# A gated delta rule in a hybrid decoder block: the block inverses leave through ScalarE's queue, the first chunk's apart and first

## The chip, the cores and the metric

One core of a Trainium2 chip runs one program. The metric is the device time of one execution in microseconds (us), median of several runs, lower is better. The core's engines are TensorE (PE), VectorE (DVE), ScalarE (ACT), GpSimd (POOL) and SyncE (SP); SyncE computes nothing and issues transfers. Each engine works through its own queue in order.

## What is computed

One decoder block in float32 for 1024 tokens of 1024 features. The normed input goes through one projection; one group of heads does sparse attention, the other the gated delta rule; both results go through an output projection, a second norm, a gated feed-forward layer and a last norm. The change touches the delta rule. The reference, cut to that part (chunks of 64 tokens there):

```python
a = jnp.where(strict, jnp.einsum('nbhcd,nbhed->nbhce', kb, k) * decay, 0.0)
tmat = lax.linalg.triangular_solve(a + eye, eye, left_side=True, lower=True, unit_diagonal=True)
u = tmat @ (v * beta[..., None])
w = tmat @ (kb * jnp.exp(gc)[..., None])
def step(S, xs):
    q_i, k_i, u_i, w_i, gc_i, qk_i = xs
    v_new = u_i - w_i @ S
    o = (q_i * jnp.exp(gc_i)[..., None]) @ S + qk_i @ v_new
    S = S * jnp.exp(g_last) + jnp.einsum('bhck,bhcv->bhkv', k_i * jnp.exp(g_last - gc_i)[..., None], v_new)
    return S, o
```

The triangular inverse `tmat` of each chunk must be there before the chunk's first step; the state `S` makes the steps a chain over the chunks.

## The kernel before

The kernel works with 8 chunks of 128 tokens and 4 heads, so 32 triangular matrices of 128 x 128. They are inverted in two stages. First the 32 x 32 blocks on their diagonals, 4 in each of 32 matrices, are inverted all at once: each of the 128 partitions holds one block. Then each chunk's blocks are joined to a 128 x 128 inverse by TensorE.

The order in the source is this. `gdn_proj` projects and convolves q, k and v feature block by feature block and writes them to `gD` in DRAM. `gram(c)` makes a chunk's triangular matrices and writes them to `gaD`, and the masked products of q and k to `gqD`. Then comes the inversion of the diagonal blocks: `bd` is read back from `gaD` through `diag_view`, which puts one block on each partition; 31 rounds of two VectorE operations (L574, L576) build the inverse in `xi`; `xi` is written to `uD` (L577); VectorE copies it transposed into a second tile under the tag "bd" (L579); that goes to `tD` (L580). Each row of 32 numbers is one run of 128 bytes in DRAM, so each of the two writes has 4096 runs. `uD` and `tD` were filled with zeros before (L398), 4 writes each, so that the parts off the diagonal read as zero. All these transfers are issued by SyncE.

The scan has two classes. `Inv.load(c)` reads a chunk's `u0` and `t0` (L636, L637) and then three pieces of `gaD` (L640, L643); `i1` to `i4` join the blocks, and `i1` (helper line L617) needs `t0`. `Scan.s0(c)` reads q, k (L503) and v (L686), transposes v and k with 8 matmuls (L625) and scales them with 8 ScalarE copies (L691, L697). `s1` to `s4` are the chunk's step, `rest` its output. `ORDER` interleaves the stages of chunk c with the inverse of chunk c + 1, and `seq` chains their matmuls in that order on TensorE. For chunk 0 the source has the load, `i1` to `i4`, and after them `s0`.

What runs beside it: projections for the attention heads (`proj_tok`), written after the scan in the source, fill TensorE while the inversion runs. A projection takes 8 token blocks of 24 matmuls; each block ends in one of 2 PSUM banks "mm", ScalarE evicts it (L812 for keys, L827 for queries) into one of 2 tiles "kst", GpSimd rotates it (L317 to L322), SyncE writes it out (L814 to `kD`, L829 to `qD`). New weights come through `wprep` (L203 read, L205 ScalarE copy, L208 GpSimd remainder).

The order on each engine is not the source's: the framework builds the queues ahead of the run by playing the program through with estimated times, taking what is ready and, of several, what stands first in the source. A wait at the head of a queue holds everything behind it. Tiles of a pool take addresses that earlier pools gave back; a tile waits for the tiles that lay there. Before, `xi`, `bd` and `tmp` lie in the pool `pg` on the left side, whose place the scan's pool `ph` takes when `pg` closes.

Of the kernel before, what the change touches and what calls it, by code (L numbers as in the profile page):

```python
# [79 lines left out]
def hybrid_block(ctx, tc, xT, xN, pos, cst_d, vec_d, w_tok, w_gdn, cw1, cw2, cpos, w_out, w_gu, w_dn, out):  # L80
# [7 lines left out]
    def mk(pool, shape, tag, dtype=F32, bufs=1):  # L88
        return pool.tile(list(shape), dtype, name=nm(tag), tag=tag, bufs=bufs)

    def pool(name, side=None, space=None):
        st = ExitStack()
        kw = {} if space is None else {"space": space}
        p_ = st.enter_context(tc.tile_pool(name=name, bufs=1, side=side, reuse_waits="tile", **kw))
        return p_, st
# [4 lines left out]
    def bc(ap, shape):  # L100
        return ap.to_broadcast(list(shape))
# [31 lines left out]
    def dram(shape, tag):  # L133
        return mk(dr, shape, tag)
# [2 lines left out]
    gD = dram([12, P, T], "gD")  # L137
    zD = dram([NT, P, 512], "zD")
    gaD = dram([NT * 4, HS], "gaD")
    uD = dram([NT * 4, HS], "uD")  # L140
    tD = dram([NT * 4, HS], "tD")
    gqD = dram([NT, P, 4, P], "gqD")
    mgD = dram([P, 2, 4, T], "mgD")
    kD = dram([NT, P, 256], "kD")
# [6 lines left out]
    def chunk_view(d, c):  # L151
        return d[c * 4:(c + 1) * 4, 0:P * P].rearrange("h (s t) -> s h t", t=P)

    def diag_view(d):
        return bass.AP(tensor=d.tensor, offset=d.offset, ap=[[HS // 4, P], [P, 32], [1, 32]])


    pc = ctx.enter_context(tc.tile_pool(name="pc", bufs=1))
# [233 lines left out]
    zz = mk(p1, [P, 1032], "zz")  # L392
    G.memset(zz, 0.0)
    for d in (uD, tD):
        zv = d.rearrange("(p a) (b f) -> p (a b) f", a=1, b=4)
        zv = bass.AP(tensor=d.tensor, offset=d.offset, ap=[[4 * 1032, P], [1032, 4], [1, 1032]])
        for b in range(4):
            dma(zv[:, b, :], zz)  # L398
    p1_x.close()
    psa_x.close()  # L400

# [160 lines left out]
    V.scalar_tensor_tensor(out=fv, in0=ssk, scalar=0.5, in1=rk, op0=ALU.mult, op1=ALU.mult)  # L562


    bd = mk(pg, [P, 32, 32], "bd")
    dma(bd, diag_view(gaD))
    xi = mk(pg, [P, 32, 32], "xi")
    G.memset(xi, 0.0)
    G.memset(xi.rearrange("p a b -> p (a b)")[:, 0:1024:33], 1.0)
    for r in range(31):  # L570
        n = 31 - r
        tmp = mk(pg, [P, 256], "tmp", F32, 2)
        tv = tmp[:, 0:(r + 1) * n].rearrange("p (a b) -> p a b", b=n)
        V.tensor_tensor(out=tv, in0=bc(xi[:, 0:r + 1, r:r + 1], [P, r + 1, n]),  # L574
                        in1=bc(bd[:, r:r + 1, r + 1:32], [P, r + 1, n]), op=ALU.mult)
        V.tensor_tensor(out=xi[:, 0:r + 1, r + 1:32], in0=xi[:, 0:r + 1, r + 1:32], in1=tv, op=ALU.subtract)  # L576
    dma(diag_view(uD), xi)  # L577
    xt = mk(pg, [P, 32, 32], "bd")
    V.tensor_copy(xt, xi.rearrange("p a b -> p b a"))  # L579
    dma(diag_view(tD), xt)  # L580
    pg_x.close()


    ph, ph_x = pool("ph")
# [45 lines left out]
    class Inv:  # L630


        def load(self, c):
            self.u0, self.t0 = pt4("u0", 3), pt4("t0", 2)
            self.b1, self.n1 = b1s[c % 2], n1s[c % 2]
            dma(self.u0, chunk_view(uD, c))  # L636
            dma(self.t0, chunk_view(tD, c))  # L637
            gv = chunk_view(gaD, c)
            for i in (0, 2):
                dma(self.b1[32 * i:32 * i + 32, :, 32 * i + 32:32 * i + 64],  # L640
                    gv[32 * i:32 * i + 32, :, 32 * i + 32:32 * i + 64])
            self.b2 = mk(ph, [64, 4, 64], "b2", F32, 2)
            dma(self.b2, gv[0:64, :, 64:128])  # L643

        def i1(self):
            p_ = bank("a")
# [139 lines left out]
    def stage(d, c, name, *a_):  # L786
        if 0 <= c < NT:
            if c not in d:
                d[c] = (Inv if d is iv else Scan)()
            return getattr(d[c], name)(*a_)  # L790

    stage(iv, 0, "load", 0)
    for n_ in ("i1", "i2", "i3", "i4"):
        stage(iv, 0, n_)
    stage(sc_, 0, "s0", 0)
    S = None
    ORDER = "s0s1 i1i1 s1s0 i1i2 s0s2 s-rest i1i3 s0s3 s0s4 i1i4"
    ORDER = [(v[0], {"0": 0, "1": 1, "-": -1}[v[1]], v[2:]) for v in ORDER.split()]
# [31 lines left out]
        return f  # L830

    ph_x.close()
    pgs_x.close()
    pk, pk_x = pool("pk", side="right")
    pt_, pt_x = pool("pt")
# [835 lines left out]
```

## Time and profile before

| | us |
|---|---|
| median of 3 runs | 1527.14 |
| lowest and highest of them | 1525.47 and 1530.09 |
| the profiled execution, own time | 1519.93 |
| its span, first to last instruction | 1518.2 |
| mean granted TensorE clock in it | 0.978 of full speed |

The profile is that of one execution. Busy time and idle time of an engine come from it, and so do the releasers: what an engine waited for, inferred from semaphores. PEclk is the clock that the throttle granted to TensorE, as a share of full speed. A transfer's time "to landing" runs from its issue. Times of single instructions are given from the start of the span.

### The profile page before, as it was taken

The page shows a single profiled execution, that of the slowest core. Times are in us where ns is not written, and L with a number is a line of the kernel's source. Part 1 is how long each engine was busy: PE and PEld are TensorE (multiplying, and loading weights), DVE is VectorE, ACT ScalarE, POOL GpSimd, SP SyncE. Part 2 cuts the span into 40 slices and gives each one's busy share as a digit, 9 for nine tenths or more (in the row PEclk, how much of TensorE's full clock was granted, in tenths as well). Part 3 has the DMA queues.
Part 4 walks back from the last instruction along what each step waited for, and adds up shares of the span by engine and source line. Part 5 has one row for each costly group of instructions (what it writes and reads, how often), then busy time and mean ns, then how long its engine had stood idle before and what let it go on. Part 6 is the DMA issues. An engine that isn't in the chain of part 4 may idle for free.

```text
span 1518.2 us, 23412 instructions
## 1 busy us (share of the span) xinstructions
PE 1432.3 (94%) x7956; PEld 1218.4 (80%) x7956; DVE 980.8 (65%) x2287; ACT 724.2 (48%) x1601; POOL 721.3 (48%) x757
## 2 busy tenths in 40 slices
PE   8989999989898999999999799999999999999997
PEld 7978877989896887888776678888888887888886
DVE  4236788827535898999857765444444443999955
ACT  5423356246545988877745443333333332344423
POOL 1222235611432665554546476666566563345445
PEclk9999999999998999999999899999999999999999
DMA  8812355398526213110145132222222227544003
GB/s 267 302 40 90 98 173 169 96 216 236 172 92 216 74 53 102 46 43 22 49 147 186 36 108 87 84 84 84 84 84 84 82 79 242 202 153 132 1 1 111
DMA packets 143031, 175.48 MB, mean 116 GB/s; under 512 B 26944, under 2 KB 79424, under 8 KB 142784
## 3 DMA queue, kind: packets, MB, share of 16 engines
q1 hardware_dynamic: 142912, 173.99, 36.7%
q8 instruction: 63, 1.03, 0.3%
q14 instruction: 56, 0.46, 0.1%
HBM read 122.54 MB, written 51.41 MB: 115 GB/s over the span
## 4 chain that ended last, share of the span: by engine, by line
PE 58%; DVE 15%; ACT 5%; DMA 3%; issue 3%; POOL 3%; SPq 0%; DVEq 0%; ACTq 0%; POOLq 0%
PE mm L119 16%; PE mm L121 16%; PE mm L120 16%; PE c L1043 2%; DVE PT L1066 2%; PE b L1063 2%; ACT Ps L1014 1%; PE a L610 1%; DVE cy L429 1%; PE a L617 1%; DMA vT<-gD 1%; DVE tmp L574 1%; PE a L997 1%; DVE xi L576 1%; ACT PT L1065 1%
## 5 line engine op out<-in xcount | busy, mean ns | idle before, releaser
L1196 POOL TENSOR_TENSOR A<-wq,A 128x512 fp32r<-128x512 f32 x94 | 126.9, 1353 | 100.9 <-ACT A L1195 92.5
L1195 ACT ACTIVATE A<-wq 128x512 fp32r<-128x512 f32 x97 | 60.9, 630 | 139.4 <-PE mm L121 121.3
L119 PE MATMUL mm<-w,xh 128*128 128x256 f32 x384 | 111.1, 289 | 9.3 <-ACT kst L827 6.2
L1066 DVE TENSOR_TENSOR PT<-b,PT 128x512 fp32r<-128x512 f32 (+2 forms) x168 | 103.8, 621 | 18.5 <-ACT PT L1065 17.3
L1196 POOL TENSOR_TENSOR wk<-wq,wk 128x512 fp32r<-128x512 f32 x64 | 85.3, 1333 | 59.0 <-ACT wk L1195 51.9
L120 PE MATMUL mm<-w,xh 128*128 128x256 f32 x384 | 110.3, 287 | 1.0 <-POOL w L208 1.0
L121 PE MATMUL mm<-w,xl 128*128 128x256 f32 x384 | 110.0, 287 | 0.0
L1065 ACT ACTIVATE PT<-b 128x512 fp32r<-128x512 f32 (+2 forms) x168 | 88.5, 537 | 38.0 <-PE b L1063 33.8
L208 POOL TENSOR_TENSOR w<-wraw,w 128x512 fp32r<-128x512 f32 x48 | 63.8, 1345 | 57.6 <-ACT w L205 55.5
L1043 PE MATMUL c<-PT,vs 128*128 128x256 f32 x528 | 90.6, 297 | 0.0
L119 PE MATMUL mm<-T,A 128*128 128x512 f32 x208 | 83.7, 403 | 4.7 <-DVE ring L1397 3.6
L120 PE MATMUL mm<-T,A 128*128 128x512 f32 x208 | 83.5, 401 | 0.0
L121 PE MATMUL mm<-T,A 128*128 128x512 f32 x208 | 83.3, 401 | 0.0
L119 PEld LDWEIGHTS mm<-w,xh 128*128 128x128 f32 x384 | 74.6, 194 | 10.0 <-ACT kst L827 6.4
L1195 ACT ACTIVATE wk<-wq 128x512 fp32r<-128x512 f32 x65 | 40.6, 629 | 88.0 <-PE mm L121 80.0
L119 PE MATMUL mm<-xh,w 128*128 128x512 f32 x192 | 75.6, 394 | 0.0
L120 PEld LDWEIGHTS mm<-w,xh 128*128 128x128 f32 x384 | 74.6, 194 | 1.2 <-POOL w L208 1.2
L121 PE MATMUL mm<-xh,w 128*128 128x512 f32 x192 | 75.2, 392 | 0.0
L1444 DVE TENSOR_TENSOR B<-B,mm 128x512 f32<-128x512 f32 x100 | 63.5, 678 | 17.5 <-PE mm L121 17.3
L120 PE MATMUL mm<-xl,w 128*128 128x512 f32 x192 | 74.8, 389 | 0.0
L121 PEld LDWEIGHTS mm<-w,xl 128*128 128x128 f32 x384 | 74.6, 194 | 0.1
L1043 PEld LDWEIGHTS c<-PT,vs 128*128 128x128 f32 x528 | 71.7, 189 | 2.3 <-DVE PT L1066 0.3
(457 smaller groups left out, 4518.5 us busy)
## 6 DMA issues: line engine op xcount, KB each, us to landing
wq<-in_w_gu SPq DMA_DIRECT2D x94, 256.0 KB, 2.7
aD<-ring SPq DMA_DIRECT2D x44, 256.0 KB, 2.2
ring<-aD SPq DMA_DIRECT2D x44, 256.0 KB, 5.3
raw<-in_w_dn SPq DMA_DIRECT2D x36, 256.0 KB, 4.5
qk<-gD SPq DMA_DIRECT2D x16, 512.0 KB, 4.7
wraw<-in_w_out SPq DMA_DIRECT2D x28, 256.0 KB, 2.8
wraw<-in_w_tok SPq DMA_DIRECT2D x24, 256.0 KB, 3.0
wraw<-in_w_gdn SPq DMA_DIRECT2D x24, 256.0 KB, 2.9
```

The source lines that it names most:

```text
L119: mm(ps, lhsT=lh, rhs=rh, start=first, stop=False, skip_group_check=grow)
L120: mm(ps, lhsT=lh, rhs=rl, start=False, stop=False, skip_group_check=grow)
L121: return mm(ps, lhsT=ll, rhs=rh, start=False, stop=last, skip_group_check=grow)
L208: (lo or G).tensor_tensor(out=wt[:, 1, k0:k0 + n, :], in0=raw, in1=f32(wt[:, 0, k0:k0 + n, :]), op=ALU.subtract)
L429: V.scalar_tensor_tensor(out=y, in0=cr[:, j:j + 512], scalar=cw[:, j:j + 1], in1=y, op0=ALU.mult, op1=ALU.add)
L1043: mm(po[:, 0:256], lhsT=v, rhs=PT[0:K, a, b_ * 256:(b_ + 1) * 256], start=(n_ == 0 and a == 0), stop=(last and b_ == len(vs) - 1 and a == 1))
L1063: tpose(pt[:, o_:o_ + P], src[:, hh, b * P:(b + 1) * P], ident)
L1065: act(out=PT[0:K, 0, 0:w], in_=pt[0:K, 0:w], func=AF.Copy)
L1066: V.tensor_tensor(out=PT[0:K, 1, 0:w], in0=pt[0:K, 0:w], in1=f32(PT[0:K, 0, 0:w]), op=ALU.subtract)
L1195: act(out=dst[:, 0], in_=src, func=AF.Copy)
L1196: after(eng.tensor_tensor(out=dst[:, 1], in0=src, in1=f32(dst[:, 0]), op=ALU.subtract), prev)
L1444: V.tensor_tensor(out=out_, in0=a_, in1=b_, op=op)
```

## The change

The inverses' writes are issued by ScalarE, no longer by SyncE, and the transposing copy moves from VectorE to ScalarE. `uD` and `tD` are each cut in two DRAM tensors: one for chunk 0 (16 of the 128 partitions) and one for the other seven; the order is u of chunk 0, the copy, t of chunk 0, the rest of t, the rest of u. The zeros are written in 16 pieces, not 8. For chunk 0 the reads from `gaD` and the whole of `Scan.s0(0)` stand ahead of the inversion in the source, and the reads of `t0` and `u0` come after it, `t0` first; for the other chunks these two reads come after those from `gaD`. `bd`, `xi` and `tmp` move to a pool of their own on the right side, so the pool `pg` ends and `ph` begins ahead of the inversion; the memsets of the tiles b1 and n1 (L588) come ahead of it with that. The area that the program reserves for descriptors of transfers issued by GpSimd is set to 1024 bytes a partition.

```diff
-    uD = dram([NT * 4, HS], "uD")
-    tD = dram([NT * 4, HS], "tD")
+    uD = [dram([4, HS], "uD0"), dram([NT * 4 - 4, HS], "uD1")]
+    tD = [dram([4, HS], "tD0"), dram([NT * 4 - 4, HS], "tD1")]
...
+    def inv_view(d, c):
+        return chunk_view(d[1], c - 1) if c else chunk_view(d[0], 0)
+
+    def diag_view(d, n=P):
+        return bass.AP(tensor=d.tensor, offset=d.offset, ap=[[HS // 4, n], [P, 32], [1, 32]])
...
-        for b in range(4):
-            dma(zv[:, b, :], zz)
+        for k, n in ((0, 16), (1, P - 16)):
+            for b in range(4):
+                dma(bass.AP(tensor=d[k].tensor, offset=d[k].offset + 1032 * b, ap=[[4 * 1032, n], [1, 1032]]), zz[0:n])
...
-    bd = mk(pg, [P, 32, 32], "bd")
+    pbd, pbd_x = pool("pbd", side="right")
+    bd = mk(pbd, [P, 32, 32], "bd")
     dma(bd, diag_view(gaD))
...
-    dma(diag_view(uD), xi)
-    xt = mk(pg, [P, 32, 32], "bd")
-    V.tensor_copy(xt, xi.rearrange("p a b -> p b a"))
-    dma(diag_view(tD), xt)
     pg_x.close()
+
+    def invert():
...
+        adma = nc.scalar.dma_start
+        xt = mk(pbd, [P, 32, 32], "bd")
+        adma(diag_view(uD[0], 16), xi[0:16])
+        act(out=xt, in_=xi.rearrange("p a b -> p b a"), func=AF.Copy)
+        adma(diag_view(tD[0], 16), xt[0:16])
+        adma(diag_view(tD[1], P - 16), xt[16:P])
+        adma(diag_view(uD[1], P - 16), xi[16:P])
...
-            dma(self.u0, chunk_view(uD, c))
-            dma(self.t0, chunk_view(tD, c))
             gv = chunk_view(gaD, c)
...
+            if c == 0:
+                sc_[0] = Scan()
+                sc_[0].s0(0)
+                invert()
+            dma(self.t0, inv_view(tD, c))
+            dma(self.u0, inv_view(uD, c))
...
-    stage(sc_, 0, "s0", 0)
...
-    nc = _bacc.Bacc("TRN2", target_bir_lowering=False, num_devices=1)
+    nc = _bacc.Bacc("TRN2", target_bir_lowering=False, num_devices=1, dynamic_dma_scratch_size=1024)
```

## Rows read from the trace of the kernel before

**Rows 1.** The page's busy times (share, instructions), by engine.
```profile
PE 1432.3 (94%) x7956; PEld 1218.4 (80%) x7956; DVE 980.8 (65%) x2287; ACT 724.2 (48%) x1601; POOL 721.3 (48%) x757
```

**Rows 2.** Windows of TensorE: length, busy (instructions), granted clock, DMA share, GB/s.
```profile
264.00:303.00 39.00, 36.61 (x289) 1.00 0.36 101
...
304.50:311.70 7.20, 1.05 (x9) 0.84 1.43 206
311.70:316.50 4.80, 4.78 (x24) 0.53 0.91 254
316.50:326.90 10.40, 10.39 (x94) 1.00 0.75 219
...
341.00:351.50 10.50, 10.22 (x94) 1.00 0.82 227
```

**Rows 3.** Timeline of TensorE: start, length, line, operation, idle before and its releaser.
```profile
311.72 0.58 PE L119 MATMUL mm<-w,xh 128*128 128x256 f32 x1 [6.16 <-ACT kst L827]
...
316.31 0.89 PE L617 MATMUL a<-t,b 128*128 128x64 f32 x7
```

**Rows 4.** The chain that ended last, 303 to 312 us: start, length, what.
```profile
303.19 2.37 DVE bd L579
...
306.08 5.00 DMA qD<-kst
```

**Rows 5.** Timeline of SyncE's queue: issues, their start and length.
```profile
303.19 0.37 SPq L577 DMA_DIRECT2D uD<-xi  x1
305.59 0.39 SPq L580 DMA_DIRECT2D tD<-bd  x1
306.08 3.14 SPq L829 DMA_DIRECT2D qD<-kst  x2
```

**Rows 6.** Timeline of ScalarE: evictions of the query projection's token blocks.
```profile
297.09 0.47 ACT L827 ACTIVATE kst<-mm,rstd 128x256 f32<-128x256 f32 x1 [0.85 <-PE mm L121]
299.97 0.47 ACT L827 ACTIVATE kst<-mm,rstd 128x256 f32<-128x256 f32 x1 [2.41 <-PE mm L121]
311.19 0.47 ACT L827 ACTIVATE kst<-mm,rstd 128x256 f32<-128x256 f32 x1 [10.74 <-DMA qD<-kst]
```

**Rows 7.** Timeline of GpSimd: rotation, weights' remainders, memsets.
```profile
296.32 4.05 POOL L208 TENSOR_TENSOR w<-wraw,w 128x512 fp32r<-128x512 f32 x3
...
301.37 0.32 POOL L322 TENSOR_TENSOR kst<-rp,rp 128x64 f32<-128x64 f32 x1
...
302.80 0.99 POOL L588 MEMSET b<- 128x512 f32 x2
```

**Rows 8.** Groups of ScalarE, 264 to 396 us, by shape: busy, mean ns.
```profile
L205 ACT ACTIVATE w<-wraw 128x512 fp32r<-128x512 f32 x8 | 4.7, 621 | 3.3 <-DMA wraw<-in_w_tok 3.3
```

**Rows 9.** Transfers (count, KB each, median us to landing).
```profile
qD<-kst SPq DMA_DIRECT2D x16, 128.0 KB, 1.7
...
t<-tD SPq DMA_DIRECT2D x8, 256.0 KB, 4.8
vT<-gD SPq DMA_DIRECT2D x8, 256.0 KB, 3.0
...
tD<-bd SPq DMA_DIRECT2D x1, 512.0 KB, 5.2
```

**Rows 10.** The chain in time, at chunk 0's eight transposes.
```profile
322.22 0.87 PE b L625 x8
```

**Rows 11.** Timeline of VectorE: steps of the inversion.
```profile
296.21 0.34 DVE L576 TENSOR_TENSOR xi<-xi,tmp 128x175 f32<-128x175 f32 x1
296.59 1.30 DVE L574 TENSOR_TENSOR tmp<-xi,bd 128x156 f32<-128x156 f32 x1
```

**Rows 12.** Timelines of SyncE (last zero writes, next read) and TensorE.
```profile
66.10 4.94 SPq L398 DMA_DIRECT2D tD<-zz  x4
71.14 1.60 SPq L203 DMA_DIRECT2D wraw<-in_w_gdn  x1
...
104.72 0.50 PE L119 MATMUL mm<-xh,w 128*128 128x512 f32 x1
```

More of the change, by code (lines that the diff above doesn't have):

```diff
@@ L152, in chunk_view @@
         return d[c * 4:(c + 1) * 4, 0:P * P].rearrange("h (s t) -> s h t", t=P)
-    def diag_view(d):
-        return bass.AP(tensor=d.tensor, offset=d.offset, ap=[[HS // 4, P], [P, 32], [1, 32]])
+    def inv_view(d, c):
+        return chunk_view(d[1], c - 1) if c else chunk_view(d[0], 0)
+    def diag_view(d, n=P):
+        return bass.AP(tensor=d.tensor, offset=d.offset, ap=[[HS // 4, n], [P, 32], [1, 32]])
     pc = ctx.enter_context(tc.tile_pool(name="pc", bufs=1))
@@ L394, in hybrid_block @@
     for d in (uD, tD):
-        zv = d.rearrange("(p a) (b f) -> p (a b) f", a=1, b=4)
-        zv = bass.AP(tensor=d.tensor, offset=d.offset, ap=[[4 * 1032, P], [1032, 4], [1, 1032]])
-        for b in range(4):
-            dma(zv[:, b, :], zz)
+        for k, n in ((0, 16), (1, P - 16)):
+            for b in range(4):
+                dma(bass.AP(tensor=d[k].tensor, offset=d[k].offset + 1032 * b, ap=[[4 * 1032, n], [1, 1032]]), zz[0:n])
     p1_x.close()
@@ L562, in hybrid_block @@
     V.scalar_tensor_tensor(out=fv, in0=ssk, scalar=0.5, in1=rk, op0=ALU.mult, op1=ALU.mult)
-    bd = mk(pg, [P, 32, 32], "bd")
+    pbd, pbd_x = pool("pbd", side="right")
+    bd = mk(pbd, [P, 32, 32], "bd")
     dma(bd, diag_view(gaD))
-    xi = mk(pg, [P, 32, 32], "xi")
+    xi = mk(pbd, [P, 32, 32], "xi")
     G.memset(xi, 0.0)
     G.memset(xi.rearrange("p a b -> p (a b)")[:, 0:1024:33], 1.0)
[L570 to L576, printed above, removed]
-    dma(diag_view(uD), xi)
-    xt = mk(pg, [P, 32, 32], "bd")
-    V.tensor_copy(xt, xi.rearrange("p a b -> p b a"))
-    dma(diag_view(tD), xt)
-    pg_x.close()
+    pg_x.close()
+    def invert():
+        for r in range(31):
+            n = 31 - r
+            tmp = mk(pbd, [P, 256], "tmp", F32, 2)
+            tv = tmp[:, 0:(r + 1) * n].rearrange("p (a b) -> p a b", b=n)
+            V.tensor_tensor(out=tv, in0=bc(xi[:, 0:r + 1, r:r + 1], [P, r + 1, n]),
+                            in1=bc(bd[:, r:r + 1, r + 1:32], [P, r + 1, n]), op=ALU.mult)
+            V.tensor_tensor(out=xi[:, 0:r + 1, r + 1:32], in0=xi[:, 0:r + 1, r + 1:32], in1=tv, op=ALU.subtract)
+        adma = nc.scalar.dma_start
[5 more added lines that the diff above has]
+        adma(diag_view(uD[1], P - 16), xi[16:P])
     ph, ph_x = pool("ph")
@@ L832, in hybrid_block @@
     ph_x.close()
+    pbd_x.close()
     pgs_x.close()
```

## The prediction, made before the changed kernel ran

> **What bounds the kernel now.** I read the page's busy times first: TensorE works 94% of the span [rows 1], so a change pays here only by the TensorE idle time that it takes away. Then the windows of TensorE around the inversion. Up to 303 us it is nearly full; from 304.5 to 311.7 it does 1.05 us of work; in the next 4.8 us it works through 24 matmuls at a granted clock of 0.53, which is the lower of its two levels (1.2 GHz); after that it is full at 1.00, and a chunk of the scan fills 10.22 of 10.5 us [rows 2]. So the scan itself is TensorE's own work, and the hole in front of it is what can be won. The reader is to see its size: one stop of 6.16 us [rows 3], and one token block (24 matmuls) that took 316.31 - 311.72 = 4.6 us at the lower clock, against a rhythm of 2.88 us between evictions (297.09 to 299.97) [rows 6]. Together 6.2 + 1.7 = 7.9 us, 0.5% of the run.
>
> The chain of waits says who made the hole [rows 4]: VectorE's transposing copy ends near 305.56, then a write of q (qD<-kst) takes 5.00 us, then ScalarE evicts a bank (L827), then TensorE goes on. SyncE's queue says why that write was late [rows 5]: it stands behind the two inverse writes (L577, L580), which wait for VectorE, and it issued at 306.08, though GpSimd had finished its tile (L322, starts 301.37 and takes 0.32) at 301.69 [rows 7]. Two kst tiles and two PSUM banks then hold up everything behind.
>
> **The sum.** It is made against the profiled execution, 1519.93 us (span 1518.2), which is 7.2 us under the median of the three runs; the difference is put on the median.
>
> 1. Inverse writes leave SyncE. The q write can issue at 301.7, not 306.08, so the eviction of the third token block needs no 10.74 us wait. What now ends last is the data of the first chunk, steps 2 to 4.
> 2. ScalarE, after the last VectorE step at 303.19 (not moved): issue of the first u piece, 0.37 as at L577 [rows 5]; the copy of 1024 elements a partition. No such ScalarE copy is in the trace. Bounds: 1.24 (twice the 0.62 of a 512-element copy, L205, [rows 8]) and 2.37, the VectorE copy it replaces [rows 4]. I take 1.24, since it is the same engine and function. The t piece issues at 303.19 + 0.37 + 1.24 = 304.8 (before: 305.59).
> 3. Its landing. The whole write took 5.2; a 128 KB write of long rows took 1.7 [rows 9]. The piece holds an eighth of the bytes: 1.7 + 3.5/8 = 2.1; ends 1.7 and 5.2. Landed at 306.9.
> 4. SyncE's read of the first t0: median 4.8 [rows 9], as before beside heavy traffic (the 448 KB pieces are in flight). Ends 3.0 (another 256 KB read, vT) and 5.2 (the whole write's time). 306.9 + 4.8 = 311.7, when the scan's first matmuls (L617) can start: 316.31 - 311.7 = 4.6 earlier.
> 5. The 8 transposes of v and k for chunk 0, with their ScalarE copies, came at 322.05 to 322.9, in the full stretch, and held 0.87 us of TensorE there [rows 10, 2]. They now run before the inverse is ready and push the token blocks 0.87 into the wait that step 4 leaves. +0.9. Their eight ScalarE copies (2.3 us) fall where ScalarE stands 2.41 us ahead of each eviction [rows 6]: 0. Their reads move ahead too (qk, vT and three gaD reads of chunk 0, five issues); on SyncE they fall in a stretch in which the blocks' weights are on chip: 0, and if they came late, the transposes would only go back to where they are now.
> 6. Behind ScalarE's first write stand the copy, three more issues (0.37 to 0.39 each) and then the eviction of token block 3: 303.19 + 0.37 + 1.24 + 3 x 0.39 = 306.0, plus 0.47 [rows 6]. Block 5 can run 306.5 to 309.4, inside the wait of step 4: 0. Ends: 0, and 2.9 if the scan's first matmuls stand ahead of it in TensorE's order. I take 0, as before the whole block stood ahead.
> 7. The four memsets of the b1 and n1 tiles move from 302.80 into the inversion. VectorE's steps rose from 0.34 to 1.30 while GpSimd ran L208 [rows 7, 11]. Ends: 0 and 4 x 0.5 = 2.0 later. The nearest row is the transposing copy itself, which ran beside all four memsets: at the rate of a step (175 elements in 0.34) its 1024 elements ask 2.0, and it took 2.37 [rows 4]. I take that 0.4: -0.4. The Trainium skill, SBUF — State Buffer, section "Who interferes with whom", says that a VectorE instruction with two SBUF inputs is held up by a GpSimd instruction that reads SBUF, not by one that only writes; by that rule the memsets would cost 0 and the sum be 0.4 larger, and the 1.30 beside L208 agrees with it.
> 8. Zeroing in 16 writes instead of 8: 8 more issues on SyncE near 66 us, at 1.2 each (4.94 for four) at most 10 us later for the w_gdn reads, which start at 71.14 [rows 12]. TensorE first uses them at 104.72, so some 20 us of cover stay. 0. If that cover were gone, the same 10 us would be TensorE's. The smaller descriptor area and the moved tiles: 0; no transfer in the trace is issued by GpSimd.
>
> Sum: 4.6 + 0.9 - 0.4 = 5.1 us, of the 7.9 that are there: 1527.14 - 5.1 = **1522.0**. About 0.3% (4.6 us) is what a measurement of this kernel can tell from no change.
>
> **Rivals.**
> *A, the first piece lands no sooner than the whole did.* The four pieces follow each other within 1.2 us on one queue and share the engines with each other and with the reads, whose share of DMA time in the hole was 1.43 [rows 2]. Landing then takes 5.2: 304.8 + 5.2 + 4.8 = 314.8, won 1.5 + 0.9 - 0.4 = 2.0, or **1525.1**. For it: the 128-byte rows, slow in both whole writes. Against it: the t piece is second on an empty queue, ahead of the big ones. The Trainium skill, DMA: Bandwidth & Descriptors, "Rules for kernel authors", says that two transfers to disjoint partition halves serialize and should be one; read strictly the split gives nothing, and then the sum would be this rival's. No row here shows a split write.
>
> *B, ScalarE stops instead of SyncE (slower).* Its queue is in order too. If the first inverse write stands ahead of the evictions that ran at 297.09 and 299.97, both banks fill and TensorE stops at 299.97, 6 us sooner. ScalarE comes free after four issues at 306.0; one issue behind two large writes can take 2.7 more (the two q writes at 306.08 took 3.14 together, [rows 5]), so 306.0 to 308.7, and TensorE does three blocks ahead of the scan, one of them at the low clock: 0.5 + 4.6 + 2 x 2.9, i1 at 316.9 to 319.6, and 2.7 more if a second issue is held up. Minus the 0.9 of step 5: -0.3 to +5.1, about +3: **1530**. It decides from the point where that write sits before the eviction of 299.97. For it: the builder orders by estimated times, and before it put both inverse writes ahead of a q write that was ready at 301.69, while VectorE ended at 303.19; its estimate is early by 1.5 us or more. Against it: 1.5 us early is still behind 299.97.
>
> *C, all of the hole closes.* The piece takes 1.7 and the read 3.0, as vT's: the scan starts at 304.8 + 1.7 + 3.0 = 309.5, won 6.8 + 0.9 = 7.7, **1519.4**; TensorE then stands for no more than about a microsecond.
>
> **How the numbers follow.** Forecast (won 3 to 7) 0.40, of which 0.31 lies over 4.6; A 0.22; B 0.24, a third of it beyond +4.6; C 0.10; 0.04 for queues that the builder orders worse further on. Faster 0.31 + 0.10 = 0.41; same 0.09 + 0.22 + 0.16 = 0.47; slower 0.08 + 0.04 = 0.12. The forecast's own range is 1520 to 1524. With A, C and most of B, and with some 2 us by which single runs lie off their median (1525.47 to 1530.09 around 1527.14), it is 1516 to 1531.
>
> **What would show it.** Right: qD<-kst (L829) issues near 302; the first L617 matmul at 311 to 312, with its v and k transposes before it; the stop of TensorE under 3 us and no window of clock 0.53. A shows as a t piece of some 5 us to landing; B as an eviction L827 waiting for a VectorE step, and a TensorE stop that begins near 300. The prediction is wrong in its reasons if the hole stays with another releaser, or if it closes and the time doesn't follow; the place to look is then the end of the scan.

## The result, and the profile after

The changed kernel takes **1540.78 us** (median of 7 runs, 1538.46 to 1547.6) against 1527.14 (7 runs beside it, 1524.4 to 1533.5): a ratio of **1.0088, 95% interval 1.0064 to 1.0112**. It is slower by 13.6 us. The profiled execution of it has a span of 1539.6 us; that is 21.4 over the profiled span of before, of which some 7 are the luck of the profile of before, which lies that far under its median.

Windows of TensorE of the kernel after; the first one reaches from the read of the blocks of A (bd<-gaD) to the first matmul of attention (a<-ksw,QS), the others cut the part around the inversion (length, busy, count, granted clock, DMA share, GB/s):

```profile
270.77:484.30 213.53, 193.91 (x1557) 0.91 0.52 147
272.00:284.00 12.00, 8.85 (x63) 0.86 0.85 200
284.00:300.00 16.00, 12.32 (x79) 0.79 0.66 207
309.90:316.70 6.80, 0.48 (x3) 0.60 1.20 270
316.70:338.70 22.00, 22.00 (x109) 0.50 0.28 78
338.70:350.00 11.30, 11.30 (x105) 1.00 0.65 187
```

The same window of the kernel before, from its bd read to its first attention matmul:

```profile
266.75:464.41 197.66, 182.71 (x1557) 0.98 0.57 159
```

These two long windows hold the loss: 213.5 against 197.7, 15.9 of the 21.4 us. The rest is 4.0 before the bd read and 1.5 behind the window. In both, the profile has the same 1557 matmuls. They stand still 19.6 us rather than 15.0, and they are busy 193.9 us rather than 182.7: **4.7 us went into stops and 11.2 us into the same matmuls at a lower clock**. In [rows 2] TensorE worked 4.8 us at the low clock, and that was over before the scan; here the clock is at 0.50, TensorE's lower level (1.2 GHz), for the first 22 us of the scan, in which TensorE is busy all the time. From the first inversion matmul to the first transposes of `on` the first chunk takes 29.1 us (316.7 to 345.8), before 21.8 (316.3 to 338.1).

TensorE's stops in the timeline after, which answer to [rows 3] (start, length, line, operation, idle before and releaser):

```profile
281.29 1.09 PE L634 MATMUL b<-cst,vT 128*128 128x128 f32 x4 [3.15 <-DMA vT<-gD]
294.52 0.58 PE L119 MATMUL mm<-w,xh 128*128 128x256 f32 x1 [3.68 <-ACT kst L824]
309.88 0.39 PE L119 MATMUL mm<-w,xh 128*128 128x256 f32 x1 [2.24 <-ACT kst L824]
316.70 1.94 PE L626 MATMUL a<-t,b 128*128 128x64 f32 x8 [6.32 <-DMA t<-tD]
```

The stop of 6.16 for an eviction tile is gone, and one of 6.32 is there, for t, right ahead of the first inversion matmul (L626, L617 before). The 2.24 us ahead of it are for an eviction (L824, 309.35) that stands behind the inverse writes in ScalarE's queue. The chain after says why t was late; it answers to [rows 4]:

```profile
305.18 0.35 ACTq L586
305.58 0.03 ACT bd L587
305.61 4.97 DMA uD<-xi
310.59 0.37 SPq L656
311.01 1.10 SPq L656
312.21 4.35 DMA t<-tD
316.70 1.51 PE a L626 x6
```

The two queues show the order behind it. First ScalarE's timeline, then SyncE's (in place of [rows 5, 6]):

```profile
290.53 0.72 ACT L778 ACTIVATE zth<-zt,hr 128x512 f32<-128x512 f32 x1 [5.94 <-DMA zt<-zD]
294.00 0.84 ACT L824 ACTIVATE kst<-mm,rstd 128x256 f32<-128x256 f32 x2 [2.74 <-DMA kD<-kst]
305.58 2.08 ACT L587 ACTIVATE bd<-xi 128x1024 f32<-128x1024 f32 x1 [3.05 <-DVE xi L582]
305.61 0.46 ACTq L590 DMA_DIRECT2D uD<-xi  x1
307.70 1.01 ACTq L588 DMA_DIRECT2D tD<-bd  x1
309.35 0.84 ACT L824 ACTIVATE kst<-mm,rstd 128x256 f32<-128x256 f32 x2 [1.68 <-issue]
```

```profile
285.52 0.43 SPq L774 DMA_DIRECT2D zt<-zD  x1
287.59 3.37 SPq L826 DMA_DIRECT2D kD<-kst  x2
307.98 4.14 SPq L656 DMA_DIRECT2D u<-uD  x3
312.21 0.60 SPq L655 DMA_DIRECT2D t<-tD  x1
312.90 0.93 SPq L826 DMA_DIRECT2D kD<-kst  x2
```

L590 is the rest of u (448 KB). The text of the program puts it last; the builder issued it ahead of t's first piece. SyncE took the u reads of chunks 0, 1 and 2 ahead of chunk 0's t, and the second of them waits for that rest. And only 24.1 token blocks (of 24 matmuls) stand ahead of the scan in TensorE's program order, before 28.9: no query block is among them, and the first eviction of one (L839) starts at 366.23, before at 297.09.

### The profile page after: what moved, and what is told of

Read it like the earlier page. It is cut to its first block, busy times and chain, and to the rows that moved or that the text cites. A ratio compares the mean times of both kernels' runs of the same rounds, so it can differ in the third digit from the quotient of the medians.

```text
span 1539.6 us, 23423 instructions
## 1 busy us (share of the span) xinstructions
PE 1447.8 (94%) x7956; PEld 1232.9 (80%) x7956; DVE 977.5 (63%) x2286; ACT 727.2 (47%) x1602; POOL 720.9 (47%) x757
## 4 chain that ended last, share of the span: by engine, by line
PE 60%; DVE 13%; ACT 5%; issue 4%; POOL 3%; DMA 2%; SPq 0%; POOLq 0%; ACTq 0%; DVEq 0%
PE mm L119 16%; PE mm L121 16%; PE mm L120 16%; PE c L1056 3%; DVE PT L1079 2%; PE b L1076 2%; PE a L626 2%; PE a L619 1%; ACT Ps L1027 1%; DVE cy L431 1%; PE a L1010 1%; ACT PT L1078 1%; DVE ring L1342 1%; DMA mgt<-mgD 1%; DVE Pw L964 1%
## 5 line engine op out<-in xcount | busy, mean ns | idle before, releaser
L119 PE MATMUL mm<-w,xh 128*128 128x256 f32 x384 | 112.9, 294 | 7.1 <-ACT kst L824 5.9
L120 PE MATMUL mm<-w,xh 128*128 128x256 f32 x384 | 112.6, 293 | 1.0 <-POOL w L211 1.0
L119 PEld LDWEIGHTS mm<-w,xh 128*128 128x128 f32 x384 | 76.4, 199 | 7.9 <-ACT kst L824 6.3
L120 PEld LDWEIGHTS mm<-w,xh 128*128 128x128 f32 x384 | 76.5, 199 | 1.3 <-POOL w L211 1.2
L431 DVE SCALAR_TENSOR_TENSOR cy<-cr,vec,cy 128x512 f32<-128x512 f32 x72 | 62.8, 872 | 17.3 <-POOL cr L424 5.9
```

The costliest lines, as they stand in the source:

```text
L119: mm(ps, lhsT=lh, rhs=rh, start=first, stop=False, skip_group_check=grow)
L120: mm(ps, lhsT=lh, rhs=rl, start=False, stop=False, skip_group_check=grow)
L431: V.scalar_tensor_tensor(out=y, in0=cr[:, j:j + 512], scalar=cw[:, j:j + 1], in1=y, op0=ALU.mult, op1=ALU.add)
```

## The experiments

The kernel before ran beside each batch (medians 1527.6 to 1529.3). All runs in one table: ratio to the kernel before with its interval, and of the profiled execution the window from the bd read to attention, TensorE's busy time in it, and the stop right ahead of the first inversion matmul. Busy time includes unused matmuls in the five runs marked *.

| run | ratio | interval | window | busy | stop |
|---|---|---|---|---|---|
| before | 1 | | 197.7 | 182.7 | 0 |
| after | 1.0088 | 1.0064–1.0112 | 213.5 | 193.9 | 6.3 |
| e1_scratch | 0.9981 | 0.9959–1.0003 | 199.3 | 185.3 | 0 |
| e2_zeros16 | 1.0013 | 0.9989–1.0037 | 201.1 | 186.2 | 0 |
| e4_sp_writes | 1.0034 | 1.0013–1.0055 | 200.3 | 186.2 | 1.4 |
| e5_act_only | 1.0003 | 0.9982–1.0024 | 198.1 | 184.1 | 0.8 |
| e6_s0_back | 1.0081 | 1.0054–1.0108 | 209.2 | 189.7 | 6.3 |
| e7_t0_first | 1.0081 | 1.0055–1.0108 | 207.3 | 189.7 | 3.1 |
| e8_clock_held * | 1.0075 | 1.0048–1.0103 | 214.7 | 200.6 | 3.0 |
| e9_zt_late | 1.0101 | 1.0077–1.0125 | 212.9 | 192.1 | 7.0 |
| e10_clock_held12 * | 1.0044 | 1.0029–1.0059 | 204.3 | 193.3 | 0 |
| e11_before_kst4 | 0.9993 | 0.9975–1.001 | 202.1 | 186.9 | 7.0 |
| e12_after_kst4 | 1.0074 | 1.006–1.0089 | 211.2 | 193.0 | 6.0 |
| e13_tiles_only | 1.0059 | 1.004–1.0078 | 210.6 | 193.2 | 5.1 |
| e14_loads_late | 1.0056 | 1.0036–1.0076 | 209.4 | 192.5 | 7.1 |
| e15_sp_hold * | 0.9988 | 0.9969–1.0007 | 198.6 | 186.1 | 0 |
| e16_kst4_hold * | 1.0001 | 0.9981–1.0021 | 199.4 | 191.2 | 0 |
| e17_sp_kst2 | 1.0031 | 1.0012–1.005 | 201.5 | 185.7 | 0 |
| e17_sp_kst3 | 0.9994 | 0.9975–1.0013 | 197.5 | 183.6 | 0 |
| e18_tiles_hold * | 1.0014 | 0.9994–1.0033 | 204.8 | 191.5 | 0 |

### Which part costs

**e1_scratch**: `num_devices=1` becomes `num_devices=1, dynamic_dma_scratch_size=1024`, in the kernel before.

> The kernel before with the smaller descriptor area alone. My theory is that the loss of the change (13.6 us) comes from the order of SyncE's queue around the inversion (about 10 us: reads of chunks 0 to 2 that the earlier pool lets in stand ahead of the key writes, token blocks stop, TensorE falls to its lower clock for the first chunk) and from the 16 zero writes (about 4 us). By it this run lies within 2 us of before: 1525 to 1529. If the descriptor area matters by itself: 1532 or more.

Measured 1524.8 us, 0.9981: no cost.

**e2_zeros16**: the kernel before, with the zeros in sixteen writes.

```
-        for b in range(4):
-            dma(zv[:, b, :], zz)
+        for p0, p1_ in ((0, 16), (16, P)):
+            for b in range(4):
+                dma(zv[p0:p1_, b, :], zz[0:p1_ - p0])
```

> The kernel before with 16 zero writes instead of 8, nothing else. My theory: the w_gdn reads behind them come some 6 us later on SyncE, ScalarE's copies of those weights stand ahead of the evictions that the key compression needs, and the first gated-delta projection starts 3 to 5 us later (108 to 109 instead of 104.7): 1529 to 1532. The rival, that the shift seen there is chance or comes from the builder's order of the whole program: within 1.5 us of before.

1530.94 us, 1.0013, by itself no difference that can be told. It lies 0.3% above e1, but the intervals overlap: about 5 us, give or take as much.

**e4_sp_writes**: the changed kernel, its writes from SyncE and its copy on VectorE.

```
-        adma = nc.scalar.dma_start
+        adma = dma
...
-        act(out=xt, in_=xi.rearrange("p a b -> p b a"), func=AF.Copy)
+        V.tensor_copy(xt, xi.rearrange("p a b -> p b a"))
```

> The changed kernel with the inverse writes issued by SyncE again, and the transposing copy on VectorE; tiles, reads, pieces and zeros as changed. My theory (order of the reads on SyncE): still 8 to 14 us above before, 1535 to 1541, with key writes delayed by several us after 280 and a long stretch of lower clock in the first chunk. The rival (ScalarE stopped by its writes is the cause): only the zeros' cost is left, 1528 to 1532.

1534.78 us, 1.0034, between the two theories. The early reads, transposes and tiles stayed, and more than half of the loss went. In its profile the stop ahead of the scan is 1.4 us; that execution (1526.36 us) is the fastest of ten and lies 8.4 under their median, so it need not show what the median lost.

**e5_act_only**: the changed kernel's writes, copy, pieces and zeros with the tiles in the old pool and the reads and transposes where they were (t read ahead of u).

```
-    pbd, pbd_x = pool("pbd", side="right")
...
+    invert()
+    pg_x.close()
...
+    stage(sc_, 0, "s0", 0)
```

> The writes of the change (ScalarE's queue, four pieces, copy on ScalarE, 16 zero writes), with the tiles in their old pool, the reads of u0 and t0 ahead of the gaD reads and Scan.s0(0) in its old place. In its queue the first write stands ahead of the evictions of the first two query blocks. My theory: the key writes go out in time; zeros +4, the stop of ScalarE costs 0 to +3: 1529 to 1534. The rival (ScalarE's stop is the cause): 1538 or more, with a stop of TensorE that begins near 300 and lasts 7 us or more.

1529.45 us, 1.0003. With the tiles in their old place ScalarE's queue costs nothing that can be told: the new stop is there (5.41 us for an eviction, L836), but it takes the place of the old one, with token blocks behind it. With the tiles moved it does cost: between the changed kernel and e4, which differ by ScalarE's part alone, lie 0.54%, with intervals that do not meet.

**e13_tiles_only**: the kernel before with the tiles on the right and the old pool closed before the inversion, and the scratch that makes room.

```
+    pbd, pbd_x = pool("pbd", side="right")
-    bd = mk(pg, [P, 32, 32], "bd")
+    bd = mk(pbd, [P, 32, 32], "bd")
...
+    pg_x.close()
     for r in range(31):
...
-    pg_x.close()
```

> The kernel before with one part of the change alone: the blocks' tiles on the right, the older pool closed before the inversion (with the scratch that makes room); writes, order in the text, zero writes and evictions as before. Theory 'the builder's order': the free space lets the builder put the first chunks' other reads ahead of the key writes on SyncE and the first tanh among the key evictions on ScalarE, and 27.0 rather than 28.9 token blocks ahead of the scan; TensorE shows a new stop ahead of 300 us, and the time is 1529 to 1534. Theory 'ScalarE's writes make the loss': nothing moves, 1524 to 1528.

1536.87 us, **1.0059**, more than was expected: the tiles' move alone loses two thirds as much as the whole change, with the inverse writes where they always were. Its windows, from the bd read to attention, the stop ahead of the scan, and what follows it:

```profile
271.00:481.60 210.60, 193.22 (x1556) 0.92 0.54 149
312.00:317.10 5.10, 0.03 (x1) 0.69 0.96 275
317.10:334.70 17.60, 17.13 (x84) 0.51 0.36 104
```

It is the picture of the changed kernel: a stop, then the scan at the lower clock, and 7.9 us more busy time than in e1_scratch, which has the same scratch.

**e14_loads_late**: e13 with every read into the scan's pool ordered behind the write of t.

```
+    t_write = dma(diag_view(tD), xt)
...
-            dma(zt, zD[c])
+            after(dma(zt, zD[c]), t_write)
```

> The run with the tiles alone moved (ratio 1.0059 to the kernel before), with one order added: every read into the scan's pool stands behind the write of t on SyncE's queue, as it did in the kernel before, where the memory was not free sooner; the tiles lie as in that run. Theory 'the free memory lets the builder reorder': the early reads, the tanh among the key evictions and the stop ahead of 300 us go, some 28 blocks stand ahead of the scan as before, and the time comes back to 1524 to 1529, a ratio of 0.998 to 1.001. Rival 'the place of the tiles itself': the stops and the time stay, 1534 to 1539.

1538.32 us, 1.0056: the theory that the early reads are the loss fell. The stops ahead of 300 us did shrink to one of 2.4, but now TensorE stood 7.1 us ahead of the scan. Windows as above, and SyncE's timeline:

```profile
270.30:479.70 209.40, 192.48 (x1555) 0.93 0.54 150
310.40:317.60 7.20, 0.12 (x2) 0.71 1.10 169
317.60:340.60 23.00, 21.61 (x106) 0.50 0.62 179
```

```profile
308.21 1.65 SPq L584 DMA_DIRECT2D tD<-bd  x1
311.69 0.94 SPq L639 DMA_DIRECT2D u<-uD  x1
312.72 0.93 SPq L643 DMA_DIRECT2D b<-gaD  x2
314.65 0.38 SPq L640 DMA_DIRECT2D t<-tD  x1
```

28.0 blocks stand ahead of the scan here; they end at 310.5. In the kernel before it is one more, the block that waited for an eviction tile and ran from 311.72 to 316.31 at the low clock [rows 3]; its tile came free through the query writes, issued right behind the inverse writes [rows 5]. Here the builder issues all those reads first and the first query write only at 394.87, and puts that block behind the scan's first matmuls. So the tiles' move changes the whole order, query writes and token blocks with the reads, and not the early reads alone. The rival's figure, for the place of the tiles, did come; no run moves the tiles without also ending the old pool earlier, so which of the two tips the builder's order is open.

### The order of the queues

**e6_s0_back**: the changed kernel, the first chunk's transposes behind its inversion again.

```
-                sc_[0] = Scan()
-                sc_[0].s0(0)
...
+    stage(sc_, 0, "s0", 0)
```

> The changed kernel with one part undone: the first chunk's transposes and key scaling stand again behind its block inversion (the early reads of the blocks of A, the tiles on the right, the ScalarE writes and the sixteen zero writes stay). The changed kernel is 13.6 us over the one before by the medians (1540.8 against 1527.1). Theory 'stops and the clock behind them': ahead of the inversion's end TensorE stops 3.15 us for vT and 3.68 us for a key eviction, and the stretch 272 to 300 has granted clocks of 0.86 and 0.79 (some 4.5 us); without the transposes ahead the first stop goes and the second shrinks, so 1533 to 1537. Theory 'the t0 read': the loss sits behind 305 us alone, so 1539 to 1541.

1537.86 us, 1.0081. The stop for vT went, the waits for eviction tiles grew from 5.9 to 9.1 us, and the 6.3 ahead of the scan stayed. Neither theory's figure can be told from the other here; the transposes are at most a small part.

**e7_t0_first**: the changed kernel with the order that the text asks for made binding.

```
+        t_rest = adma(diag_view(tD[1], P - 16), xt[16:P])
+        after(adma(diag_view(uD[1], P - 16), xi[16:P]), t_rest)
...
+            after(dma(self.u0, inv_view(uD, c)), t0_read[0])
```

> The changed kernel with two orders added and nothing else: the rest of u is written behind the rest of t on ScalarE's queue, and each read of u stands behind the first read of t on SyncE's. In the changed kernel the order came out the other way, the second read of u waited for 448 KB, and the first read of t was issued only at 312.2 us. Theory 'the order of the queues': the first read of t is issued at 309 to 310, the first inversion matmul comes at 313.5 to 315 rather than 316.7, the stop before it falls from 6.3 to some 3 us and the stretch of low clock behind it shortens, so 1532 to 1536. Theory 'the transposes and reads ahead': the loss was made before 300 us, and this gives 2 us at most, so 1538 to 1540.

1538.67 us, 1.0081. The stop fell from 6.3 to 3.1 us as foreseen, but the clock fell all the same, 1.9 us into the scan, which began at 314.88, and came back at 330.5:

```profile
314.80:316.80 2.00, 1.11 (x8) 1.00 1.28 266
316.80:330.50 13.70, 12.85 (x65) 0.50 0.43 123
```

The busy time stayed at 189.7 us, 4 to 7 more than in e1_scratch and before. Half of the stop kept most of the price.

**e9_zt_late**: the changed kernel, the gate's reads behind the first read of t (`after(dma(zt, zD[c]), t0_read[0])`).

> The changed kernel with one order added: the reads of the output gate's blocks stand behind the first read of t, so that the first tanh (L778, which waited 5.9 us for its read) no longer stands ahead of the key evictions on ScalarE. Theory 'stops and the clock behind them': TensorE's stop of 3.68 us at 294.5 goes and the clock in 284 to 300 comes back in part, so 1534 to 1537. Rival 'SyncE holds the keys': the two eviction tiles come free no sooner, because the key writes stand behind the early reads on SyncE, the stop stays at 3 to 4 us and the time at 1539 to 1541.

1542.94 us, 1.0101: no gain. The rival was right: with the tanh gone the eviction still waited (3.55 us).

### The clock

**e8_clock_held**: six unused matmuls ahead of the first inversion matmul of the changed kernel.

```
+            if self is iv[0]:
+                hold = bank("a")
+                for _ in range(6):
+                    after(mm(hold, lhsT=ident, rhs=xts[0]...[:, 0:512], start=True, stop=True), seq[0])
```

> The changed kernel with six matmuls added that compute nothing that is used (128x512 of float32, some 5 us in all), right ahead of the first inversion matmul, in the 6.3 us that TensorE stands for the first read of t. Theory 'stops and the clock behind them': in the changed kernel the granted clock is 0.50 to 0.58 from 310 to 340 us, which costs 10.9 us; with TensorE busy in the stop the rows after it show 0.9 to 1.0, and the time falls to 1530 to 1533. Theory 'the clock falls by the scan's own small matmuls': the rows from 318 stay at 0.5 and the time stays at 1539 to 1542.

1539.38 us, 1.0075. They ran as soon as their data was there and left 2.98 us of stop, so the clock fell anyway: 0.50 from 317 to 339. The run says nothing on a held clock.

**e10_clock_held12**: the same with twelve.

```
-                for _ in range(6):
+                for _ in range(12):
```

> The changed kernel with twelve rather than six unused matmuls (128x512 of float32, 0.74 us each in the run with six) ahead of the first inversion matmul. With six, TensorE still stood 2.98 us before that matmul, the clock fell to 0.50 just as the scan began and stayed there until 339 us, so that run did not test what a held clock is worth; twelve, some 8.9 us from 308.8, reach over the arrival of t at 316.8. Theory 'a stop right ahead of the scan': with no stop the granted clock stays at 1.00 from 316 to 340, which gives back about 10.9 us and costs about 1, so 1530 to 1533 by the median, a ratio of 1.002 to 1.004 to the kernel before. Theory 'the scan's own small matmuls lower the clock': it falls to 0.50 within some us of 318 all the same, 1539 to 1542.

1534.52 us, **1.0044**, a little over the 1.002 to 1.004 expected: half of the loss is back. (The profiled execution, 1539.94 us, is the slowest of six; its bd read came 5.3 us later than in the changed kernel.) Windows from the bd read to attention, of the unused matmuls, and of the scan behind them:

```profile
276.10:480.40 204.30, 193.31 (x1579) 0.97 0.55 153
312.50:323.00 10.50, 10.50 (x26) 1.00 1.04 218
323.00:343.00 20.00, 20.00 (x182) 1.00 0.50 134
```

The scan's matmuls, 182 in 20 us, begin at the full clock (2.4 GHz) and keep it. In the changed kernel 109 went through in 22 us.

**e18_tiles_hold**: e13 with eight unused matmuls, in i1 of the first chunk.

```
+            if self is iv[0]:
+                hold = bank("a")
+                for _ in range(8):
+                    after(mm(hold, lhsT=ident, rhs=flat(n1s[0]), start=True, stop=True), reads[0])
```

> The run with the tiles alone moved (ratio 1.0059, a stop of 5.1 us right ahead of the first inversion matmul, then 0.50 of clock until 334.8 us, 14.7 us lost to the clock between the first block read and attention) with eight unused matmuls of 0.85 us in that stop. Theory 'the low clock behind a stop right ahead of the scan': the clock holds at 1.00 through the scan's first chunk and the ratio falls to 1.001 to 1.003. Rival 'the token blocks that the builder put behind the scan': those are lost either way, and the ratio stays at 1.005 to 1.007.

1530.57 us, **1.0014** after 1.0059: three quarters of the tiles' cost is the clock behind that one stop.

```profile
269.00:473.80 204.80, 191.51 (x1573) 0.97 0.55 153
309.00:318.20 9.20, 9.20 (x38) 1.00 1.11 261
318.20:340.00 21.80, 20.70 (x186) 1.00 0.53 153
```

**e11_before_kst4** and **e12_after_kst4**: four tiles for the evicted blocks rather than two, in the kernel before (with the scratch) and in the changed one.

```
-        kt = mk(pw, [P, 256], "kst", F32, 2)
+        kt = mk(pw, [P, 256], "kst", F32, 4)
```

> The kernel before with four rather than two tiles for the evicted key and query blocks (and the scratch of 1024 that makes room for them, which by itself gave a ratio of 0.998). TensorE no longer stops 6.16 us for an eviction tile at 305.6; but the same 28.9 blocks stand ahead of the first inversion matmul and t arrives no sooner. Theory 'a stop right ahead of the scan': TensorE runs out of blocks at some 311 to 313 and stops 3 to 5 us for t, the clock falls as the scan begins, and the stretch after it runs at 0.5 for 10 to 20 us: 1531 to 1536, slower than before by 0.3 to 0.5%, although the wait that bounded the stage is gone. Theory 'stops alone': the time falls by the stop and its clock, or at worst stays: 1520 to 1527.

> The changed kernel with four rather than two tiles for the evicted blocks, nothing else. The builder then puts 26.1 token blocks ahead of the first inversion matmul rather than 24.1, and evictions wait less for the key writes behind the early reads. Theory 'a stop right ahead of the scan': two more blocks (5.8 us) run in the 6.3 us in which TensorE stood for t; if the stop falls under 2 us and the clock holds, the long stretch at 0.50 goes, and the time with it to 1527 to 1532; if a stop of 3 us or more is left there, the stretch stays and the time at 1536 to 1541. Rival 'early reads and transposes': the stop at 294 us alone goes, 1536 to 1538.

e11: 1527.18 us, 0.9993. The old stop went, a stop of 7.0 us stands ahead of the scan instead, and the clock is at 0.51 behind it. That was expected; the 4 to 9 us of loss were not there. Against e1_scratch, which has the same scratch and two tiles, the window is only 2.8 us longer (202.1 and 199.3), since the old stop and its low clock went in exchange; a difference of that size can't be told here. The low stretch is shorter than in the changed kernel:

```profile
266.60:468.70 202.10, 186.87 (x1557) 0.96 0.56 155
308.20:315.10 6.90, 0.02 (x1) 0.81 1.07 219
315.10:329.70 14.60, 14.60 (x73) 0.51 0.60 175
```

e12: 1539.75 us, 1.0074; two more blocks stand ahead of the scan, but TensorE stood 4.0 us for an eviction tile among them and then 6.0 for t, and the low clock stayed with it, as the expectation had it for that case.

**e16_kst4_hold**: e11 with the lines of e18 and `range(11)`.

> The kernel before with four eviction tiles (a ratio of 0.9993 by itself, with a stop of 7.0 us right ahead of the first inversion matmul and 0.50 of clock from 313 to 329 us), and eleven unused matmuls of 0.85 us in that stop. Theory 'a stop right ahead of the scan': the clock stays at 1.00, which gives back the 7.2 us that the low clock cost between the first block read and attention, less what was lost there in the kernel before: 1519 to 1524, a ratio of 0.994 to 0.998. Rival: the low clock in that stretch costs nothing by the end, since the scan's chain is bound by the other engines there: 0.999 to 1.001.

1528.03 us, 1.0001, no gain over e11, although the clock held (window of the scan):

```profile
315.60:338.00 22.40, 22.05 (x196) 1.00 0.82 236
```

The window to attention shrank by 2.7 us only: the unused work overran, the first inversion matmul came 13.9 us behind the inversion's last step rather than 11.9. The end does not show these 2.7, which lie within the intervals. The rival's figure came, but this run can't tell it from the overrun. So a held clock gave back some 7 us (0.44 and 0.45%) where the low stretch is 18 to 22 us long (e10, e18), and nothing that could be told where it is 14.6.

### The part that was meant to gain

**e17_sp_kst2**: old tiles and order of the text, four pieces from SyncE with VectorE's copy, t's first read ahead of u's. **e17_sp_kst3**: the same with three eviction tiles. **e15_sp_hold**: with four, and three unused matmuls. Against e5_act_only:

```
-        adma = nc.scalar.dma_start
+        adma = dma
...
-        act(out=xt, in_=xi.rearrange("p a b -> p b a"), func=AF.Copy)
+        V.tensor_copy(xt, xi.rearrange("p a b -> p b a"))
```

> The part of the change that does what the prediction counted on, alone: tiles and order of the text of the kernel before, block inverses in the changed kernel's four pieces, but from SyncE's queue and with the copy on VectorE; the first read of t ahead of that of u; sixteen zero writes. 28.7 token blocks stand ahead of the first inversion matmul (28.9 before). Theory 'the first chunk's piece is worth what was counted': t arrives some 2 to 3 us sooner against the inversion's end than in the kernel before (13.7 us), and 1 to 4 us of it reach the end: 1523 to 1527, a ratio of 0.997 to 0.999. Theory 'the stop for an eviction tile sets the end of the stage': the query writes stand behind four pieces rather than two on SyncE, the stop stays at 5 to 6 us, and the ratio is 0.999 to 1.002.

> The run above with three rather than two tiles for the evicted blocks (30.4 blocks ahead of the first inversion matmul, the first read of t behind three query writes). Theory: TensorE's stop for an eviction tile falls by about one block (2.9 us), with no unused matmul needed and dense blocks left behind it, so the clock is back before the scan: 1521 to 1525, a ratio of 0.995 to 0.998. Rival: the read of t behind one more query write costs what the tile wins, 0.998 to 1.001.

> A version meant to beat both: tiles and order of the text of the kernel before; the block inverses written from SyncE's queue in the changed kernel's four pieces (the first chunk's first) with the copy on VectorE; the first read of t ahead of that of u; four tiles for the evicted blocks; and three unused matmuls (128x512 of float32, 0.85 us each) right ahead of the first inversion matmul. Theory 'a stop right ahead of the scan': the stop for an eviction tile (6.2 us) is gone, t arrives some 11 us rather than 13.7 behind the inversion's end, TensorE reaches the scan with under 1.5 us of stop and the granted clock stays at 1.00 through it: 1520 to 1525, a ratio of 0.995 to 0.998. Theory 'the order of the builder decides': a new stop of 3 us or more appears ahead of the scan and the ratio is 0.999 or more.

e17_sp_kst2: 1532.38 us, 1.0031. The first chunk's piece by itself gains nothing, and SyncE's timeline says why:

```profile
311.12 0.33 SPq L585 DMA_DIRECT2D tD<-bd  x1
312.03 2.56 SPq L587 DMA_DIRECT2D uD<-xi  x1
314.70 2.93 SPq L841 DMA_DIRECT2D qD<-kst  x2
318.23 0.41 SPq L646 DMA_DIRECT2D t<-tD  x1
```

t's piece is issued at 311.12, but its read stands behind the rest of u and two query writes and issues 7.1 us later; the stop for an eviction tile stays at 6.2. With three tiles the stop falls to 3.3 and the time to 1526.95 us, 0.9994; e15 gives 1526.85, 0.9988. e17_sp_kst2 is slower than the kernel before by 0.31%; the other two can't be told from it. Nothing that was tried beats it.

## Why the prediction was wrong

**The sign.** It forecast 1522 us, with 0.12 for slower. Only its last remainder, queues that the builder orders worse, has to do with what came.

**The hole and its reader (first part): right in size, wrong in price.** The hole of 6.2 us was priced with 1.7 for the clock. What a stop costs depends on what stands behind it. Before, a token block stood there and took the low clock on itself, 4.6 us, and the scan began at 1.00 [rows 2]. With the scan itself behind the stop, TensorE worked 22 us at the low clock there and 9 us ahead of 300; together they took the 11.2 us.

**Step 1 failed.** The writes left SyncE, but no query write could profit: the builder put no query block ahead of the scan, and the first query write issued at 390.22.

**Steps 2 and 3 held within their bounds.** ScalarE's copy took 2.08 (taken 1.24, upper bound 2.37). That bound was VectorE's copy in the one profile in which the four memsets of GpSimd ran beside it; in the eleven other profiles with the copy on VectorE no memset did, and it took 1.11 to 1.19. So the move to ScalarE made the copy about 1 us longer. The t piece landed in 3.8 us (2.3 to 3.4 in e4, e7 and e17_sp_kst2) against 2.1. The Trainium skill, DMA: Bandwidth & Descriptors, "Rules for kernel authors", says that two transfers to disjoint partition halves serialize and one should be used; rival A was read from it. The trace agrees only in part: in the changed kernel the piece of t was there 3.8 us after its issue, and the rest of t, issued 1 us later, 5.6 us after its own; the small part is there sooner.

**Step 4 failed in its start, not its length.** The read took 4.35 (4.8 taken), but issued at 312.21, not 306.9, behind three u reads. e7 put it in order and won 3.2 us of the stop, yet little of the time.

**Step 5's "0" for the reads failed,** with stops of 3.15 and 3.68 us and clocks of 0.86 and 0.79 ahead of 300. But e6 and e9 show that mending either by itself brings back nothing that can be told.

**Step 6 is the step that failed and decided.** Its bound said one block, 2.9 us, if the scan's matmuls stood ahead of a token block in TensorE's order. They stood ahead of almost five (24.1 against 28.9). "I take 0, as before the whole block stood ahead" was the mistake: the order of before was taken as given, though the change moves tiles and frees memory earlier, and the builder plans anew. The "moved tiles: 0" at the end of step 8 is the same mistake, and e13 puts 0.59% on it. The price is not in the blocks themselves: with the clock held e18 has as few of them ahead as e13 (26.8 and 27.0) and loses 0.14% rather than 0.59. It is in the stop that comes to stand right ahead of the scan, and in the low clock behind it. That the free memory is what the builder answered to is argued, not shown (e14).

**Step 7:** the memsets ran at 269.8 to 271.7, ahead of the inversion, and held up nothing there. Their price beside VectorE's copy was probably mis-sized: 0.4 was taken, and the copy's 2.37 against 1.12 in the profiles without them makes 1.25.

**Step 8, sixteen zero writes:** the w_gdn read came at 77.42 rather than 71.14 and the first matmul of that projection at 108.58 rather than 104.72 [rows 12]. One profile shows no cause here: e13, with eight zero writes, has that matmul at 108.98. Over the twenty profiles it comes at 102.9 to 109.0 with eight (seven profiles, mean 106.2) and at 106.0 to 114.1 with sixteen (thirteen, mean 109.4), so some 3 us of the cover may be missing. In the time it is about 5 us, give or take as much (e2 against e1); e5, e15 and e17_sp_kst3 have the sixteen too and can't be told from the kernel before. Not settled.

**Rivals.** In the changed kernel the landing (3.8) was about as far from A's 5.2 as from the forecast's 2.1; it decided nothing. B saw a real stop (5.41 us in e5, 2.24 in the changed kernel), but e5 lost nothing by it. C's condition never came.

So the tiles' move alone loses 0.59% (e13), and three quarters of that is the clock behind the stop that it leaves ahead of the scan (e18); in the whole change, which loses 0.88%, holding the clock gives 0.44 back (e10). That the clock is no accident of the profiled executions, the granted clock of all of them shows: its median is 0.967 in the changed kernel (7) and 0.968 in e13 (6), but 0.973 in the kernel before (116) and e10 (6) and 0.975 in e18 (12). The parts do not add up: e4 has the moved tiles and all the rest but ScalarE's part and loses only 0.34. ScalarE's queue costs only together with the new order, by a way that no run shows. Some 0.3 is what e2 and e1 differ by; that the zero writes make as much of the loss is argued, not shown.

## What to carry to other kernels

Moving tiles so that a pool closes earlier is not a free edit where a builder orders the queues: count, on every engine's program order, what now stands ahead of the critical first instruction. A stop is to be priced with what runs behind it: the dense matmuls of a token block had the clock back after 4.5 us in the kernel before, while the scan's chain of small dependent ones ran on at the lower level for 22 us in the changed one. If a stop can't be removed, leave a dense block between it and such a chain, as the kernel before did.

## What was not expected of the hardware

The clock has a memory here. The first chunk's matmuls kept 1.00 where they began at it with no stop ahead of them (before, e10, e16, e18), and stayed at 0.50 for 14.6 to 23.0 us where they began there behind a stop of 5 to 7 us (e11, e13, after, e14), in most of these windows with TensorE shown as busy throughout. Beginning at 1.00 is not enough: in e4 and e7, with 1.4 and 3.1 us of stop ahead and shorter ones (0.5 and 1.7 us) among the first matmuls, the clock fell 4.0 and 1.9 us into the chunk. Whether it is the size of the chain's matmuls or their dependence that keeps the low level, no run separates. The matmuls show which level they had: the first eight (128x64, a<-t,b) take 1.00 us at the full clock in the kernel before and 1.94 at the lower one in the changed one. The Trainium skill, TensorE: Matmul & The Clock Gate, "HAM oscillation — how this bites in real kernels", says that a wait on a transfer throttles TensorE, and that the matmuls behind it start slow. The trace agrees with the fall; how long it lasts is told by the rows alone.
